# The gated MLP of a two-layer decoder trunk: from one interleaved pass to an up phase with seven block products per pair of chunks and a down phase fed from DRAM

## The chip, the cores and the metric

One core of a Trainium2 chip runs the kernel. The metric is the device time of one execution in microseconds (us). Five engines work side by side, each through its own queue in order: TensorE (PE in the profile; PEld is its weight load), VectorE (DVE), ScalarE (ACT), GpSimd (POOL) and SyncE (SP), which here issues nearly all DMA transfers.

## The reference

Two layers work on 1024 tokens of width 1024. Each adds attention and then the MLP to the residual stream. Only the MLP is changed:

```
def conv_ffn(xn, w_up, conv_w, conv_b, w_down):
    u = xn @ w_up                      # 1024 -> 2 * 2816
    c = conv_b
    for j in range(CONV_WIDTH):        # 3 taps, causal, per channel
        c = c + conv_w[j] * up[:, j:j + s]
    val, gate = jnp.split(c, 2, axis=-1)
    return (jax.nn.silu(gate) * val) @ w_down

h = h + conv_ffn(rmsnorm(h, norm_ffn[layer]), ...)
```

The 2816 hidden channels are 22 blocks of 128 rows. A block `j` has a value chunk and a gate chunk of `w_up`: a pair.

## The kernel before

Activations lie with channels on the 128 partitions and tokens along the free dimension, in two halves of 512 tokens. Every float32 product is made of three matmuls: each operand is split into a high part (rounded to the matmul's own format) and the remaining low part, and `hi*hi + hi*lo + lo*hi` is summed in one bank of PSUM (`mm3`, L162 to L164). A weight tile comes through `load_w`: DMA (L108), a rounding copy on ScalarE (`whi`, L109), a subtraction on GpSimd (`wlo`, L110).

`ffn_phase` runs behind `attention_phase` in each layer. It first ends the output projection of token half 1 (`out_final`, 24 matmuls), then the norm of that half, and then goes through the 22 pairs. For each pair, `up_half` makes four banks (two chunks, two token halves, 8 blocks of the inner dimension, 3 matmuls each: 96 matmuls). ScalarE and VectorE read each bank straight from PSUM for the convolution (L775, L777); two small instructions (L783) carry the two tokens across the border of the halves. `gate` (L788 to L793) applies the activation, multiplies on GpSimd and splits the product into `gh` and `gl`.

The down projection is interleaved: GROUPS (4, 4, 4, 4, 2, 4 pairs) are multiplied with their rows of `w_down` while the next group's pairs are made, and every group's result is added to the residual `h` from its bank (L259). Together 2112 up matmuls and 1056 down matmuls per layer. The order of the instructions on each queue is fixed when the program is built, by a scheduler; TensorE's order in the attention phase is that of the code.

Of the kernel before, what the change touches and what calls it, by code (L numbers as in the profile page):

```python
# [6 lines left out]
F32 = mybir.dt.float32  # L7
# [22 lines left out]
def trunk(ctx, tc, a, out):  # L30
# [60 lines left out]
    h_scr = [[dram.tile([P, HT], F32, name=f"hscr{c}_{h}") for h in range(2)] for c in range(KD)]  # L91
    c_scr = dram.tile([NMIX, T], F32, name="cscr")
# [93 lines left out]
    def mem_norm(l):  # L186
        mh = [qk(f"mh{i}").rearrange("p (k t) -> p k t", k=4) for i in range(2)]
        ml = [qk(f"ml{i}").rearrange("p (k t) -> p k t", k=4) for i in range(2)]
        macc = sqt("macc")
        mT = [tab(f"mT{i}").rearrange("p (k t) -> p k t", k=4) for i in range(2)]  # L190
        for i in range(2):
            nc.sync.dma_start(mT[i], a["memT"][:, 4 * i:4 * i + 4, :])
        for k in range(KD):
            square_acc(macc, mT[k // 4][:, k % 4, :], k == 0)
        rb = norm_rb(macc, psp, 2)
        mhk, mlk = (lambda k: mh[k // 4][:, k % 4, :]), (lambda k: ml[k // 4][:, k % 4, :])
        norm_split(lambda k: mT[k // 4][:, k % 4, :], rb, 3 * l + 1, mhk, mlk)
        return mhk, mlk
# [30 lines left out]
    H = {}  # L229
    PART = {}  # L230
    KORD = list(range(NPAIR - 2)) + [NPAIR, NPAIR + 1, NPAIR - 2, NPAIR - 1]

    def h_tiles(half):

        if half == 0:
            t = [big("h0", F32).rearrange("p a b -> p (a b)").rearrange("p (n t) -> p n t", n=4) for _ in range(2)]
            H[0] = lambda n: t[n // 4][:, n % 4, :]
        else:
            t = big("h1", F32).rearrange("p a b -> p (a b)").rearrange("p (n t) -> p n t", n=4)
            u = [yt("h1").rearrange("p (n t) -> p n t", n=2) for _ in range(2)]  # L240
            H[1] = lambda n: t[:, n, :] if n < 4 else u[n // 2 - 2][:, n % 2, :]

# [23 lines left out]
    def out_final(l, half, acc, psum):  # L266
# [3 lines left out]
        for n in range(KD):  # L270
            ps = psum(n)
            mm3(ps, lambda k: cols(hi)(n), lambda k: cols(lo)(n), lambda k: oh[:, c, :], lambda k: ol[:, c, :], 1)
            residual(ps, n, half, PART[l] if half else None)
            square_acc(acc, H[half](n), n == 0)
            yield n


    def attention_phase(l):
        with tc.manual_schedule(engines={mybir.EngineType.PE}):
# [207 lines left out]
            def out_last():  # L487
# [9 lines left out]
                x_split(0, rb, 3 * l + 2)  # L497
# [97 lines left out]
            if l == 0:  # L595
                MEM[0] = mem_norm(0)
                xn[0] = x_norm(0, x_load(0))
                next(xn[0])
# [142 lines left out]
    def ffn_phase(l):  # L741
        UP = ["s", "tp", "s", "tp", "s"]
        DN = ["p", "p", "o"]
# [4 lines left out]
        def norm_later(half, acc, gi):  # L748
            for rb in norm_stages(acc, psp):
                yield  # L750
            x_split(half, rb, gi)

        def normed(half, acc, gi):
            x_split(half, norm_rb(acc, psp), gi)


        h_tiles(1)
        acc = sqt("acc")
        run(out_final(l, 1, acc, lambda n: bank_of("all", ALL)))
        normed(1, acc, 3 * l + 2)  # L760


        up_st = {}

        def up_half(ci, half):
            if half == 0:
# [12 lines left out]
            if half == 0:
                nc.vector.tensor_copy(e, ps[:, HT - 2:])  # L780
            else:
                for d in (1, 2):
                    nc.vector.scalar_tensor_tensor(t[:, o:o + d], e[:, 2 - d:], w(2 - d), t[:, o:o + d],  # L783
                                                   op0=ALU.mult, op1=ALU.add)

        def gate(j):
            v, g = up_st.pop(2 * j)[2], up_st.pop(2 * j + 1)[2]
            nc.scalar.activation(g, g, AF.Silu)  # L788
            nc.gpsimd.tensor_tensor(v, v, g, op=ALU.mult)
            gh = qk("gh")  # L790
            gl = ptt("gl", [P, T])
            nc.scalar.copy(gh, v)  # L792
            nc.vector.tensor_tensor(gl, v, gh.bitcast(F32), op=ALU.subtract)  # L793
            return gh, gl

        def up(j):
            todo = [(2 * j + s, half) for s in range(2) for half in range(2)]
            if j == 0:
                todo = [(0, 0), (1, 0), (2, 0), (0, 1), (1, 1)]
            elif j == 1:  # L800
                todo = [(2, 1), (3, 0), (3, 1)]
            for ci, half in todo:
                up_half(ci, half)
            return gate(j)


        base = [sum(GROUPS[:i]) for i in range(len(GROUPS))]

        def down(gi, gt, last):
            G = GROUPS[gi]  # L810
            nb = 8 // G
            ws = {}

            def w_of(n, half):
                b = n // nb
                if (b, half) not in ws:
                    ws[b, half] = load_w(a["wd"][l, base[gi] + b])
                hi, lo = ws[b, half]
                o0 = (n % nb) * G
                return (lambda k: cols(hi)(o0 + k)), (lambda k: cols(lo)(o0 + k))  # L820

            def one(n, half):
                hs = slice(half * HT, half * HT + HT)
                ps = bank_of("all", ALL) if last else bank_of("dn", DN)
                whi, wlo = w_of(n, half if last else 0)
                mm3(ps, whi, wlo, lambda k: gt[k][0][:, hs], lambda k: gt[k][1][:, hs], G)
                residual(ps, n, half)

            if not last:
                for n in range(KD):  # L830
                    for half in range(2):
                        one(n, half)
                return
            for half in range(2):
                hs = slice(half * HT, half * HT + HT)
                acc = sqt("acc")
                for n in range(KD):
                    one(n, half)
                    square_acc(acc, H[half](n), n == 0)
                    if l == 0:  # L840
                        nc.sync.dma_start(h_scr[n][half], H[half](n))
# [117 lines left out]
```

## Time and profile before

| | us |
|---|---|
| median of 3 runs (2687.73 to 2691.45) | 2690.41 |
| profiled execution | 2691.43 |
| its span | 2689.6 |
| TensorE busy in the span | 2552.8 (95%) |
| VectorE, ScalarE, GpSimd busy | 1451.6, 1068.0, 889.3 |

The two MLP phases lie at about 622 to 1353 us and 1948 to 2673 us of the span; what is ahead of each is attention. Busy time of TensorE is not its time at peak, since its matmuls overlap: what counts is how many of them start per microsecond. A row that ends in "x4" merges neighbours, and its time then reaches from the first one's start to the last one's end, waits on the way included.

### The profile page before, as it was taken

Reading aid. Unit: us, or ns where it says so; the run is one execution under the profiler, and the core shown is the slowest. Engines: PE = TensorE matmul, PEld = TensorE weight load, DVE = VectorE, ACT = ScalarE, POOL = GpSimd, SP = SyncE. Lnnn points to the kernel's source line nnn. Section 1 sums busy time; section 2 is a strip of 40 time slices with the busy share of each in tenths; the row PEclk is TensorE's granted clock in tenths of the full one; section 3 lists DMA queues with packets and bytes.
Section 4 is the critical chain, followed back from the end, with each engine's and each line's share of the span. In section 5 each row is a group of like instructions: output and inputs, shape, how many; then the busy total and the mean of one; then the engine's idle time right before and its main releaser. Section 6 shows DMA issues by size and latency. Waiting matters only on the chain. (4 is left out here: it accounts for less than half of the span.)

```text
span 2689.6 us, 34661 instructions
## 1 busy us (share of the span) xinstructions
PE 2552.8 (95%) x12808; PEld 2133.6 (79%) x12808; DVE 1451.6 (54%) x2879; ACT 1068.0 (40%) x2077; POOL 889.3 (33%) x650
## 2 busy tenths in 40 slices
PE   5999999989999999999998898979999999999997
PEld 4878888767888888888777797867788888888886
DVE  7667777565424343434766767665554343433345
ACT  5555555544313131323355555554432222222222
POOL 5210101454323232323553333335443232233232
PEclk8899999999999999999999999999999999999999
DMA  5122223421111111111342222243211111111112
GB/s 169 48 83 56 73 62 99 145 67 64 54 49 48 48 47 51 52 47 63 121 121 62 71 66 62 71 127 105 71 48 48 53 49 48 47 48 51 52 47 94
DMA packets 103505, 187.26 MB, mean 70 GB/s; under 512 B 14236, under 2 KB 16924, under 8 KB 103336
## 3 DMA queue, kind: packets, MB, share of 16 engines
q1 hardware_dynamic: 102472, 184.36, 22.3%
q8 instruction: 101, 1.65, 0.3%
q10 hardware_dynamic: 864, 0.69, 0.1%
q14 instruction: 68, 0.56, 0.1%
HBM read 148.24 MB, written 15.78 MB: 61 GB/s over the span
## 5 line engine op out<-in xcount | busy, mean ns | idle before, releaser
L110 POOL TENSOR_TENSOR wlo<-wraw,whi 128x512 fp32r<-128x512 f32 x450 | 589.4, 1330 | 1402.1 <-ACT whi L109 1335.2
L162 PE MATMUL bk<-xh,whi 128*128 128x512 f32 x2112 | 860.7, 408 | 30.6 <-ACT xh L254 8.3
L163 PE MATMUL bk<-xl,whi 128*128 128x512 f32 x2112 | 836.4, 396 | 6.0 <-POOL xl L255 3.9
L164 PE MATMUL bk<-xh,wlo 128*128 128x512 f32 x2112 | 835.2, 395 | 0.9 <-POOL wlo L110 0.9
L109 ACT CAST whi<-wraw 128x512 fp32r<-128x512 f32 x450 | 268.2, 616 | 651.0 <-PE bk L163 448.2
L162 PEld LDWEIGHTS bk<-xh,whi 128*128 128x128 f32 x2112 | 404.5, 192 | 113.2 <-ACT xh L254 9.9
L164 PEld LDWEIGHTS bk<-xh,wlo 128*128 128x128 f32 x2112 | 403.4, 191 | 87.7 <-POOL wlo L110 1.7
L163 PEld LDWEIGHTS bk<-xl,whi 128*128 128x128 f32 x2112 | 404.3, 191 | 82.6 <-POOL xl L255 7.2
L777 DVE SCALAR_TENSOR_TENSOR gate<-bk,cw,gate 128x511 f32<-128x511 f32 (+1 forms) x176 | 131.2, 746 | 271.2 <-ACT gate L775 269.6
L162 PE MATMUL bk<-gh,whi 128*128 128x512 f32 x704 | 276.2, 393 | 1.2 <-DVE h L259 1.1
L163 PE MATMUL bk<-gl,whi 128*128 128x512 f32 x704 | 274.7, 390 | 0.0
L164 PE MATMUL bk<-gh,wlo 128*128 128x512 f32 x704 | 274.5, 390 | 0.0
L259 DVE TENSOR_TENSOR h<-h,bk 128x512 f32<-128x512 f32 x208 | 141.7, 685 | 236.5 <-PE bk L164 236.4
L388 ACT ACTIVATE y<-y,m 128x128 f32<-128x128 f32 (+1 forms) x192 | 149.3, 778 | 118.7 <-DVE m L384 116.6
L777 DVE SCALAR_TENSOR_TENSOR val<-bk,cw,val 128x511 f32<-128x511 f32 (+1 forms) x176 | 131.1, 745 | 114.6 <-ACT val L775 113.0
L399 DVE TENSOR_TENSOR ptl<-bk,pth 128x512 fp32r<-128x512 f32 (+3 forms) x288 | 152.5, 551 | 67.2 <-ACT pth L398 66.2
L398 ACT CAST pth<-bk 128x512 fp32r<-128x512 f32 (+3 forms) x288 | 131.2, 479 | 115.2 <-PE bk L397 113.5
L397 PE MATMUL bk<-ident,y 128*128 128x128 f32 x864 | 130.3, 278 | 31.4 <-DVE ptl L399 31.3
L162 PEld LDWEIGHTS bk<-gh,whi 128*128 128x128 f32 x704 | 132.5, 188 | 31.1 <-DVE h L259 2.7
L163 PEld LDWEIGHTS bk<-gl,whi 128*128 128x128 f32 x704 | 132.6, 188 | 27.8 <-issue 0.5
L164 PEld LDWEIGHTS bk<-gh,wlo 128*128 128x128 f32 x704 | 132.5, 188 | 27.7
L793 DVE TENSOR_TENSOR gl<-val,gh 128x1024 fp32r<-128x1024 f32 x44 | 53.9, 1226 | 175.5 <-ACT gh L792 175.5
(160 smaller groups left out, 3546.1 us busy)
## 6 DMA issues: line engine op xcount, KB each, us to landing
wraw<-in_wu SPq DMA_DIRECT2D x176, 256.0 KB, 2.8
wraw<-in_wd SPq DMA_DIRECT2D x104, 256.0 KB, 2.8
wraw<-in_wo SPq DMA_DIRECT2D x64, 256.0 KB, 2.8
wraw<-in_wq SPq DMA_DIRECT2D x56, 256.0 KB, 3.0
oscr<-fold SPq DMA_DIRECT2D x56, 128.0 KB, 2.3
oraw<-oscr SPq DMA_DIRECT2D x28, 256.0 KB, 3.7
cb<-cscr SPq DMA_DIRECT2D x12, 512.0 KB, 3.8
ropeqs<-roper SPq DMA_DIRECT2D x96, 64.0 KB, 2.0
```

The lines of the kernel that those rows point to most:

```text
L109: nc.scalar.copy(hi[:, w], raw[:, :n])
L110: nc.gpsimd.tensor_tensor(lo[:, w], raw[:, :n], hi[:, w].bitcast(F32), op=ALU.subtract)
L162: nc.tensor.matmul(ps, lhsT=whi(k), rhs=xhi(k), start=(first and k == 0), stop=False)
L163: nc.tensor.matmul(ps, lhsT=whi(k), rhs=xlo(k), start=False, stop=False)
L164: nc.tensor.matmul(ps, lhsT=wlo(k), rhs=xhi(k), start=False, stop=(last and k == nk - 1))
L259: nc.vector.tensor_tensor(H[half](n), (src or H[half])(n), ps, op=ALU.add)
L388: nc.scalar.activation(y[:, :nk], y[:, :nk], AF.Exp, bias=m[:, npc - 1:npc], scale=-1.0, accum_out=m[:, 2:3])
L397: nc.tensor.transpose(tp[:, jj, :], y[:, j * P:(j + 1) * P], ident)
L398: nc.scalar.copy(ph, tp[:, :nj, :])
L399: nc.vector.tensor_tensor(pl, tp[:, :nj, :], ph.bitcast(F32), op=ALU.subtract)
L777: nc.vector.scalar_tensor_tensor(t[:, o + d:o + HT], ps[:, :HT - d], w(2 - d), t[:, o + d:o + HT], op0=ALU.mult, op1=ALU.add)
L793: nc.vector.tensor_tensor(gl, v, gh.bitcast(F32), op=ALU.subtract)
```

## The change

The up projection becomes a phase of its own. The weight pair and the normed activations are each seen as a 2x2 block matrix: the weights by chunk (value, gate) and half of the inner dimension, the activations by half of the inner dimension and half of the tokens. The four result blocks come from seven block products (Strassen's scheme) in place of eight, so a pair takes 84 matmuls. The seven activation sums are made once per layer (`up_x0`, `up_x1`, `t_make`) and stay in SBUF as `t0` to `t6`. The seven weight sums are made for every pair (`prep`): loads, additions, and the high and low parts. The products' sums are put together from PSUM into a tile `u` of [128, 2, 1024] (`product`); the convolution reads `u`. The gated rows are written to DRAM (`g_scr`).

A second phase reads them back (`g_split`): first all 22 rows of token half 0 against `w_down` into eight open banks, then token half 1, with `w_down` loaded a second time. The residual is kept in DRAM meanwhile (`hf_scr`). TensorE's order is now that of the code in the MLP too. `mem_norm` of layer 1 moves into the second phase, loads its rows twice, and uses other buffers.

```diff
+        def prep(j):
+            r0, r1, r2 = (two(tab("araw")) for _ in range(3))
+            (a22, a11), (a21, a12) = ((t[:, 0, :], t[:, 1, :]) for t in (r0, r1))
+            for t, m, r in ((a22, 1, 1), (a21, 1, 0), (a11, 0, 0), (a12, 0, 1)):
+                nc.sync.dma_start(t, a["wu"][l, 2 * j + m, :, r * WC:r * WC + WC])
+            h0, l0 = map(two, w_set())
+            V.tensor_tensor(r2, r0, r1, op=ALU.add)
+            nc.scalar.copy(h0, r2)
+            G.tensor_tensor(l0, r2, h0.bitcast(F32), op=ALU.subtract)
+            h1, l1 = map(two, w_set())
+            nc.scalar.copy(h1, r0)
+            G.tensor_tensor(l1, r0, h1.bitcast(F32), op=ALU.subtract)
+            V.tensor_tensor(a21, a21, a11, op=ALU.subtract)
+            V.tensor_tensor(a12, a12, a22, op=ALU.subtract)
+            h2, l2 = (sb.tile([P, WC], R32, tag="wraw", name="adia", bufs=4) for _ in range(2))
+            V.tensor_tensor(a11, a11, a22, op=ALU.add)
+            nc.scalar.copy(h2, a11)
+            G.tensor_tensor(l2, a11, h2.bitcast(F32), op=ALU.subtract)
+            h3, l3 = map(two, w_set())
+            nc.scalar.copy(h3, r1)
+            V.tensor_tensor(l3, r1, h3.bitcast(F32), op=ALU.subtract)
...
+        def product(j, m, tags=ALL):
...
+            mm3(ps, cols(w[0]), cols(w[1]), t_k(x, 0), t_k(x, 1), 4)
...
+            if m in (2, 3):
+                st[m] = sqt("s")
+                nc.scalar.copy(st[m], ps)
+            elif m == 4:
+                V.tensor_tensor(u[:, 1, h0], ps, st[2], op=ALU.add)
+            elif m == 5:
+                V.tensor_tensor(u[:, 0, h1], ps, st[3], op=ALU.add)
+                G.tensor_tensor(st[3], st[3], st[2], op=ALU.subtract)
+            elif m == 1:
+                V.tensor_tensor(st[3], ps, st[3], op=ALU.add)
+            elif m == 6:
+                V.tensor_tensor(u[:, 1, h1], ps, st[3], op=ALU.add)
+                G.tensor_tensor(st[3], st[3], u[:, 1, h0], op=ALU.add)
+                G.tensor_tensor(st[3], st[3], u[:, 0, h1], op=ALU.subtract)
+            else:
+                V.tensor_tensor(u[:, 0, h0], ps, st[3], op=ALU.add)
+
+        def conv(j, s, u):
...
+            nc.scalar.activation(t, u[:, s, :], AF.Identity, bias=w(3), scale=w(2))
+            for d in (1, 2):
+                nc.vector.scalar_tensor_tensor(t[:, d:], u[:, s, :T - d], w(2 - d), t[:, d:], op0=ALU.mult, op1=ALU.add)
...
+            nc.gpsimd.tensor_tensor(v, v, g, op=ALU.mult)
+            nc.sync.dma_start(g_scr[l][j], v)
...
+    def up_x1(l, rb):
+        norm_in_place(l, 1, rb, (0, 1, 4, 5, 2, 3, 6, 7))
+        for c in range(2):
+            t_make(2, c, q(0, 1, c), q(1, 1, c), ALU.subtract, V, (V, G)[c])
...
+        prep(0)
+        h_tiles(1)
+        acc = sqt("acc")
+        run(out_final(l, 1, acc, lambda n: bank_of("all", ALL)))
+        prep(1)
+        st = norm_stages(acc, psp)
...
+        up_x1(l, rb)
...
+        for j in range(2, FFC):
+            if j + 1 < FFC:
+                prep(j + 1)
+            for i, m in enumerate((2, 4, 3, 5, 1, 6, 7)):
+                product(j, m)
+                if i == 0:
+                    gate(j - 1)
+        gate(FFC - 1)
+        def g_split(k, half, t):
+            raw = sqt("graw")
+            nc.sync.dma_start(raw, g_scr[l][k][:, half * HT:half * HT + HT])
+            nc.scalar.copy(t[:, 0, :], raw)
+            nc.vector.tensor_tensor(t[:, 1, :], raw, t[:, 0, :].bitcast(F32), op=ALU.subtract)
...
+        for gi, G in enumerate(GROUPS):
+            for k in range(G):
+                g_split(b0 + k, 0, gt[:, k, :, :])
+            for b in range(G):
+                hi, lo = load_w(a["wd"][l, b0 + b])
...
-        for gi, G in enumerate(GROUPS):
-            gts.append([])
-            for x in range(G):
-                gts[gi].append(up(j))
-                j += 1
-                if gi and x == (G - 1 if gi == len(GROUPS) - 1 else 0):
-                    down(gi - 1, gts[gi - 1], False)
```

Lines named below with L857 and above, up to L923, are those of the changed kernel: in `prep`, L857 adds `r2`, L859 makes `l0`, L863 `l1`, L865 and L866 the two differences, L869 `a11 + a22`, L871 `l2`, L874 `l3`; in `product`, L896, L898, L901, L903 and L907 are VectorE's sums for m = 4, 5, 1, 6, 7 and L899, L904, L905 GpSimd's three; L914 are the taps, L922 is the product of value and gate, L923 its DMA.

GpSimd's order in the MLP of layer 0 before: between two gate products (`val`) stand only the low parts of weight tiles, up and down.

```order
L789 TENSOR_TENSOR val_7757<-val_7757,gate_7828 128x1024
L110 TENSOR_TENSOR wlo_8121<-wraw_8122,whi_8120 128x512
L110 TENSOR_TENSOR wlo_8121<-wraw_8126,whi_8120 128x512
L110 TENSOR_TENSOR wlo_8187<-wraw_8188,whi_8186 128x512
L110 TENSOR_TENSOR wlo_8187<-wraw_8192,whi_8186 128x512
L789 TENSOR_TENSOR val_7905<-val_7905,gate_7976 128x1024
```

GpSimd's order at the same place after, over one pair: `s` and `u` belong to the pair being put together (`s_7076`), `alo` and `adia` to the weights of the pair two further on, `cv` to the gate.

```order
L899 TENSOR_TENSOR s_7076<-s_7076,s_7035 128x512
L859 TENSOR_TENSOR alo_7145<-araw_7139,ahi_7144 128x1024
L904 TENSOR_TENSOR s_7076<-s_7076,u_7061 128x512
L905 TENSOR_TENSOR s_7076<-s_7076,u_7061 128x512
L863 TENSOR_TENSOR alo_7150<-araw_7137,ahi_7149 128x1024
L871 TENSOR_TENSOR adia_7156<-araw_7137,adia_7155 128x512
L922 TENSOR_TENSOR cv_7184<-cv_7184,cv_7179 128x1024
L899 TENSOR_TENSOR s_7218<-s_7218,s_7177 128x512
```

The sums of the products and the weight parts of a later pair now stand in one queue, each waiting for the one ahead of it.

VectorE's order before, one chunk: all taps read a bank of PSUM (`bk`), only the two small border instructions read `edge`.

```order
L777 SCALAR_TENSOR_TENSOR val_7905<-bk_7917,cw_6332,val_7905 128x511
L777 SCALAR_TENSOR_TENSOR val_7905<-bk_7917,cw_6332,val_7905 128x510
L780 COPY edge_7916<-bk_7917 128x2
L777 SCALAR_TENSOR_TENSOR val_7905<-bk_7946,cw_6332,val_7905 128x511
L783 SCALAR_TENSOR_TENSOR val_7905<-edge_7916,cw_6332,val_7905 128x1
L777 SCALAR_TENSOR_TENSOR val_7905<-bk_7946,cw_6332,val_7905 128x510
L783 SCALAR_TENSOR_TENSOR val_7905<-edge_7916,cw_6332,val_7905 128x2
```

VectorE's order after, one pair in the steady part of the up phase, names as above.

```order
L874 TENSOR_TENSOR alo_7161<-araw_7138,ahi_7160 128x1024
L857 TENSOR_TENSOR araw_7281<-araw_7279,araw_7280 128x1024
L901 TENSOR_TENSOR s_7218<-bk_7235,s_7218 128x512
L865 TENSOR_TENSOR araw_7280<-araw_7280,araw_7279 128x512
L866 TENSOR_TENSOR araw_7280<-araw_7280,araw_7279 128x512
L903 TENSOR_TENSOR u_7203<-bk_7249,s_7218 128x512
L914 SCALAR_TENSOR_TENSOR cv_7321<-u_7203,cw_6400,cv_7321 128x1023
L907 TENSOR_TENSOR u_7203<-bk_7265,s_7218 128x512
L914 SCALAR_TENSOR_TENSOR cv_7321<-u_7203,cw_6400,cv_7321 128x1022
L869 TENSOR_TENSOR araw_7279<-araw_7279 128x512
L914 SCALAR_TENSOR_TENSOR cv_7326<-u_7203,cw_6400,cv_7326 128x1023
L914 SCALAR_TENSOR_TENSOR cv_7326<-u_7203,cw_6400,cv_7326 128x1022
```

Nine of these (all but the three that read `bk`) take both tensors from SBUF; L896 and L898 of the next pair, which read `bk`, follow, and then L874 again.

SyncE's order after, where the up phase ends: the reads of the gated rows stand behind the write of row 20 (`gscr0_20`).

```order
L114 DMA wraw_9738<-in_wd 128x512
L114 DMA wraw_9742<-in_wd 128x512
L997 DMA h0_10458<-hfscr0_0_0_109 128x512
L923 DMA gscr0_20_161<-cv_9571 128x1024
L997 DMA h0_10458<-hfscr0_1_0_111 128x512
L960 DMA graw_9686<-gscr0_0_141 128x512
L960 DMA graw_9690<-gscr0_1_142 128x512
L960 DMA graw_9694<-gscr0_2_143 128x512
```

Before, the queue held only weight loads at this place, and no transfer waited for a gate product.

## Rows read from the trace of the kernel before

**Rows 1.** The page's first part: busy us, share of the span, instructions.

```profile
PE 2552.8 (95%) x12808; PEld 2133.6 (79%) x12808; DVE 1451.6 (54%) x2879; ACT 1068.0 (40%) x2077; POOL 889.3 (33%) x650
```

**Rows 2.** Windows: both MLP phases and a quiet stretch of the first.

```profile
core 0: us, PE busy (x) PEld busy (x) DVE busy (x) ACT busy (x) POOL busy (x), PEclk, DMA share, GB/s
622.50:1353.20 730.70, 726.15 (x3194) 598.14 (x3194) 325.45 (x494) 214.59 (x323) 253.49 (x177) 1.00 0.18 59
660.00:1150.00 490.00, 490.00 (x2164) 405.73 (x2163) 194.54 (x294) 131.02 (x187) 156.47 (x109) 1.00 0.15 49
1947.80:2673.40 725.60, 722.88 (x3187) 596.02 (x3185) 309.81 (x470) 202.40 (x295) 236.97 (x164) 1.00 0.16 51
```

**Rows 3.** Page part 5, one operation's cost: busy, mean ns, idle before.

```profile
L110 POOL TENSOR_TENSOR wlo<-wraw,whi 128x512 fp32r<-128x512 f32 x450 | 589.4, 1330 | 1402.1 <-ACT whi L109 1335.2
...
L109 ACT CAST whi<-wraw 128x512 fp32r<-128x512 f32 x450 | 268.2, 616 | 651.0 <-PE bk L163 448.2
...
L259 DVE TENSOR_TENSOR h<-h,bk 128x512 f32<-128x512 f32 x208 | 141.7, 685 | 236.5 <-PE bk L164 236.4
...
L777 DVE SCALAR_TENSOR_TENSOR val<-bk,cw,val 128x511 f32<-128x511 f32 (+1 forms) x176 | 131.1, 745 | 114.6 <-ACT val L775 113.0
...
L793 DVE TENSOR_TENSOR gl<-val,gh 128x1024 fp32r<-128x1024 f32 x44 | 53.9, 1226 | 175.5 <-ACT gh L792 175.5
```

**Rows 4.** Groups of instructions by line, the same columns.

```profile
L789 POOL TENSOR_TENSOR val<-val,gate 128x1024 f32<-128x1024 f32 x44 | 105.7, 2402 | 90.9 <-ACT gate L788 90.9
...
L775 ACT ACTIVATE val<-bk,cw 128x512 f32<-128x512 f32 x88 | 68.2, 775 | 40.9 <-PE bk L164 40.9
...
L788 ACT ACTIVATE gate<-gate 128x1024 f32<-128x1024 f32 x44 | 46.7, 1061 | 99.2 <-DVE gate L783 99.2
...
L792 ACT CAST gh<-val 128x1024 fp32r<-128x1024 f32 x44 | 46.2, 1050 | 108.2 <-POOL val L789 108.2
...
L152 DVE SCALAR_TENSOR_TENSOR xn<-h,gains,bk 128x512 f32<-128x512 f32 x48 | 33.5, 738 | 2.1 <-DMA vk<-kmn 1.5 <-PE bk L135 0.6
```

**Rows 5.** Timeline of VectorE and GpSimd around 48 us: start us, us, instruction.

```profile
44.33 6.79 POOL L110 TENSOR_TENSOR wlo<-wraw,whi 128x512 fp32r<-128x512 f32 x4
...
45.25 8.02 DVE L145 TENSOR_TENSOR xacc<-xacc,sq 128x512 f32<-128x512 f32 x6
```

**Rows 6.** Instructions of line 783 (both inputs in SBUF): ns min/median/max, forms.

```profile
L783 DVE SCALAR_TENSOR_TENSOR val<-edge,cw,val x88: 200/930/1327, 649.4 to 2596.6; 128x1 f32<-128x1 f32 x44, 128x2 f32<-128x2 f32 x44
```

**Rows 7.** Timeline around 664 us: the two engines in the MLP itself.

```profile
648.13 2.53 POOL L110 TENSOR_TENSOR wlo<-wraw,whi 128x512 fp32r<-128x512 f32 x2 [5.52 <-ACT whi L109]
...
663.56 1.81 POOL L110 TENSOR_TENSOR wlo<-wraw,whi 128x512 fp32r<-128x512 f32 x1 [0.43 <-ACT whi L109]
...
663.00 1.22 DVE L793 TENSOR_TENSOR gl<-val,gh 128x1024 fp32r<-128x1024 f32 x1 [0.45 <-ACT gh L792]
664.14 1.25 DVE L783 SCALAR_TENSOR_TENSOR val<-edge,cw,val 128x2 f32<-128x2 f32 x1
```

**Rows 8.** Line 145 (both inputs in SBUF): ns min/median/max.

```profile
L145 DVE TENSOR_TENSOR acc<-acc,sq x56: 686/693/1649, 560.2 to 2675.0; 128x512 f32<-128x512 f32 x56
```

**Rows 9.** Page part 6, DMA issues: KB each, median us to landing.

```profile
wraw<-in_wu SPq DMA_DIRECT2D x176, 256.0 KB, 2.8
...
oraw<-oscr SPq DMA_DIRECT2D x28, 256.0 KB, 3.7
```

**Rows 10.** Page part 2, GB/s in 40 slices of the span.

```profile
GB/s 169 48 83 56 73 62 99 145 67 64 54 49 48 48 47 51 52 47 63 121 121 62 71 66 62 71 127 105 71 48 48 53 49 48 47 48 51 52 47 94
```

**Rows 11.** Timeline of TensorE after a wait of 2.55 us.

```profile
554.49 0.50 PE L162 MATMUL bk<-xh,whi 128*128 128x512 f32 x1 [2.55 <-ACT xh L410]
...
555.94 0.63 PE L162 MATMUL bk<-xh,whi 128*128 128x512 f32 x1
556.37 0.63 PE L163 MATMUL bk<-xl,whi 128*128 128x512 f32 x1
...
558.50 0.63 PE L162 MATMUL bk<-xh,whi 128*128 128x512 f32 x1
558.93 0.44 PE L163 MATMUL bk<-xl,whi 128*128 128x512 f32 x1
```

More of the change, by code (lines that the diff above doesn't have):

```diff
@@ L229, in trunk @@
     H = {}
+    HC = {}
     PART = {}
@@ L595, in attention_phase @@
             if l == 0:
-                MEM[0] = mem_norm(0)
+                run(mem_norm(0))
                 xn[0] = x_norm(0, x_load(0))
@@ L746, in ffn_phase, with w_set @@
         nc.sync.dma_start(cw, a["cw"][:, l])
[L748 to L754, printed above, removed]
+        V, G = nc.vector, nc.gpsimd
+        A = {}
+        sets = itertools.cycle("wpwpw")
+        def w_set():
+            if next(sets) == "w":
+                return (sb.tile([P, 1024], R32, tag="whi", name="ahi", bufs=3),
+                        sb.tile([P, 1024], R32, tag="wlo", name="alo", bufs=3))
+            return ptt("ahi", [P, 1024]), ptt("alo", [P, 1024])
@@ L786, in gate @@
[L786 to L804, printed above, removed]
@@ L807, in ffn_phase @@
-        base = [sum(GROUPS[:i]) for i in range(len(GROUPS))]
[L809 to L829, printed above, removed]
-                for n in range(KD):
-                    for half in range(2):
-                        one(n, half)
-                return
[L834 to L841, printed above, removed]
-                if l == 0:
-                    if half == 0:
-                        normed(half, acc, 3)
-                    else:
-                        NEXT.append(norm_later(1, acc, 3))
-                    continue
-                rb = norm_rb(acc, psp)
-                for k in range(KD):
-                    nc.vector.scalar_tensor_tensor(H[half](k), H[half](k), gains[:, 6, k:k + 1], rb,
-                                                   op0=ALU.mult, op1=ALU.mult)
-                    nc.sync.dma_start(out[:, k, hs], H[half](k))
@@ new lines, in ffn @@
+        rb = next(st)
+        product(1, 4, B6)
+        up_x1(l, rb)
+        for m in (3, 5, 1, 6):
+            for j in range(2):
+                product(j, m, B6)
+        product(0, 7)
+        prep(2)
+        gate(0)
+        product(1, 7)
+        for j in range(2, FFC):
[6 more added lines that the diff above has]
+        gate(FFC - 1)
@@ new lines, in finish, with after @@
+        def finish(n, half, ps, acc):
+            residual(ps, n, half)
+            square_acc(acc, H[half](n), n == 0)
+            if l == 0:
+                nc.sync.dma_start(h_scr[n][half], H[half](n))
+        def after(half, acc):
+            for rb in norm_stages(acc, psp):
+                yield
+            if l == 0:
+                x_split(half, rb, 3)
+                return
+            for k in range(KD):
+                nc.vector.scalar_tensor_tensor(H[half](k), H[half](k), gains[:, 6, k:k + 1], rb, op0=ALU.mult, op1=ALU.mult)
+                nc.sync.dma_start(out[:, k, half * HT:half * HT + HT], H[half](k))
@@ L862, in ffn_phase @@
+        nx = after(1, acc)
         if l == 0:
-            MEM[1] = mem_norm(1)
-        down(len(GROUPS) - 1, gts[-1], True)
+            NEXT.append(nx)
+        else:
+            run(nx)
     for l in range(2):
```

212 lines of the change are left out of this document (169 added, 43 removed).

## The prediction

> **What bounds the kernel now.** The page's busy times come first: TensorE is busy 95% of the span, VectorE 54%, ScalarE 40%, GpSimd 33% [rows 1]. Windows over the MLP say more: both phases run at the full clock, 1.00, that is 2.4 GHz, and in the quiet stretch 2164 matmuls start in 490.00 us, one each 0.2264 us [rows 2]. A layer's 3168 MLP matmuls take 717.3 us at that pace, and the phases last 730.7 and 725.6 us. So TensorE bounds the MLP almost alone, with 13 and 8 us of waiting. The other three engines are busy under half of it, and so the page shows their work as free. The change fills them, so the cost of one operation on each is read next [rows 3, 4], and then what VectorE and GpSimd do to each other [rows 5 to 8].
>
> **What it removes.** 12 of 96 matmuls in each of 44 pairs: 528 x 0.2264 = 119.5 us. A pair takes 84 x 0.2264 = 19.02 us, a layer 2904 matmuls, 657.5 us. Were everything else hidden, the MLPs would give back all of it. The border instructions (L783) and GpSimd's work for the down weights leave the up phase too, but these were hidden.
>
> **What a pair now asks of the other engines.** Durations: GpSimd 1.265 us for 512 columns (two in 2.53 [rows 7]) and 2.40 for 1024; VectorE 0.69 for 512 columns, both inputs in SBUF [rows 8], 1.23 for 1024, 0.685 when one input is a bank; a tap of 1023 columns 0.745 + 512 x 1.04 ns = 1.28, the slope from 0.69 and 1.23. ScalarE 0.62 and 1.05 per copy, 1.06 for the activation, and 0.775 + 512 x 0.85 ns = 1.21 for the start of a tap, its slope from the copies. Per pair:
> - GpSimd: `l0`, `l1`, gate product at 2.40; `l2` and three sums at 1.265: 12.26 us.
> - VectorE: two of 1.23, three of 0.69, four taps of 1.28, all with both inputs in SBUF: 9.65; five sums out of banks: 3.43.
> - ScalarE: three copies of 1.05, three of 0.62, two tap starts, the activation: 8.5.
>
> Each alone fits into 19.02 us. The trace says that the first two don't run at the same time. Around 48 us VectorE adds two SBUF tiles again and again while GpSimd makes low parts: six additions in 8.02 us, 1.34 each in place of 0.69, four subtractions in 6.79, 1.70 each in place of 1.265 [rows 5]. In the MLP itself, an instruction on one column, 0.20 us alone, takes up to 1.33 and 0.93 in the median [rows 6], ending with GpSimd's instruction, and GpSimd's 1.265 become 1.81 behind an `L793` [rows 7]. The taps that read banks and the sums out of banks show no such thing: their means stay at 0.745 and 0.685 [rows 3]. After the change all four taps read `u`, in SBUF.
>
> One exchange costs 1.70 us where the two durations add up to 1.96: 0.13 of overlap at each change of sides. So a pair's 16 such instructions need at least 12.26 + 9.65 - 16 x 0.13 = 19.8 us, more than TensorE's 19.02, if one of the two is always ready.
>
> The Trainium skill, "SBUF — State Buffer", section "Who interferes with whom", has this as an exclusive lock for the whole instruction: a VectorE instruction with two SBUF inputs against a GpSimd instruction that reads SBUF, the second waiting until the first is done. The trace agrees that they exclude each other, not quite that they do for all of both durations (1.70, not 1.96). By the rule a pair would need 21.9 us.
>
> **The loop of the steady part.** The order of the two queues decides how much is left idle. From the end of `l3` (L874), t = 0, one pair goes: GpSimd L899 to 1.1; VectorE's sum `r2`, which waits for it, to 2.2; ScalarE's copy to 3.4; VectorE's L901, L865, L866, the last one holding up GpSimd to 3.9; `l0` to 6.3; the first tap gets in ahead of L904, which ends at 8.6; L905 9.9; the last bank's sum (L907) 10.7; `l1` has started at 9.9 and ends at 12.3, the second tap waits for it, 13.4; L869 14.0; activation and copy 15.2; now GpSimd's `l2` waits for the last two taps and ends at 17.6; L896 and L898 17.6; the gate product takes 17.6 to 20.0, and `l3` of the next pair waits for that: 21.05. Each hand-over is taken at 0.09 us. Without the exclusion the same list closes in 15 us and TensorE's 19.02 would rule. I take 21.05; from below it is 19.8, from above the 21.9 and the 1.2 us in which this list leaves both idle, 23.1. TensorE waits 2.03 us a pair, mostly for a bank: its eight banks are held until L907 and ScalarE's copy behind `h2`. The loop rules from pair 3 or 4 on, 18 times a layer: 36.5 us.
>
> **The other terms, per layer.**
> - Start, 21 us (bounds 10 and 30). `up_x1` has eight normings of 0.74 [rows 4], then ten additions and ten low parts of 1024 columns, shared by VectorE and GpSimd, which must alternate. GpSimd has two additions for `t5` and `t6` queued ahead of the low part of `t2` that product 3 wants: it is ready 17.6 us after the norm, where TensorE has 2.7 us of work. Product 1 of pair 1 waits for a tile `u`, which comes free after `t5`. Pairs 0 and 1 end 59 us behind `out_final`, against 38 for their 168 matmuls. Before, half 0's chunks hid that norm.
> - `out_final` late, 4 us (0 to 6): `prep(0)` holds two of the three `whi` buffers, and its `l3` and `prep(1)`'s `l0` stand ahead of the last output weights.
> - From up to down, 9 us (2 to 15): the reads of gated rows stand behind the write of row 20 on SyncE; that write comes some 15 us after the last `l3`, and 3.7 us [rows 9], a copy and a low part follow, where TensorE ends its products 11 us after that `l3`.
> - Down phase, 3 us (0 to 20): 1056 matmuls as before. Half 0 moves 1.05 MB per 24 matmuls, 5.43 us: 193 GB/s. The highest slice shown has 169 [rows 10]; I take it as carried, since nothing there shows a limit.
>
> Moved `mem_norm` and the extra stores of `h` lie beside matmuls: 0, a few us if not. ScalarE's waits hold back only copies whose banks are counted above.
>
> **Sum.** 657.5 + 36.5 + 21 + 4 + 9 + 3 = 731 us per layer, 1462 for both, against 730.7 + 725.6 = 1456.3: 6 us more. On the profiled execution's 2691.4 that makes 2697, say 2698 (1 above the median of the runs). The gain of 119.5 is eaten by 73 of the loop, 42 of the start and the rest. What a measurement of this kernel can tell from no change is about 0.2%, 5.4 us.
>
> **The rivals.**
> - *The exclusion is absorbed.* If VectorE's turns fall into gaps that GpSimd has anyway (waiting for ScalarE's copies), the pair is TensorE's, 19.2: 36 x 1.85 = 67 us less, and 5 less at each start: 2621. For it: GpSimd is idle twice per pair in my list. Against it: 19.8 us of turns in 19.02. Faster begins at a loop of about 20.7 us. Chance 0.20.
> - *It costs all of both durations*, and the idle pieces remain: 23.1 a pair, 36 x 2.05 = 74 more: 2772, slower. For it: the median of 0.93 for an instruction of 0.20 [rows 6]. The skill's rule above would give this time. Chance 0.17.
> - *Gated rows bound the down phase*: at 169 GB/s a chunk takes 6.2 us, 0.77 x 22 x 2 = 34 more: 2732. For it: nothing before moves more. Against it: DMA is busy only 0.15 to 0.18 at 49 to 59 GB/s [rows 2]. Chance 0.09.
> - *The clock falls.* After a wait of 2.55 us, matmuls start 0.43 us apart, the 1.2 GHz level, until 558.9 [rows 11]: about eight, 1.6 us lost. One such fall in each pair, 19.02 + 1.6 = 20.6, still fits the loop; if the lower level lasts until the phase's granted clock is 0.83, a pair takes 19.02 / 0.83 = 22.9 us and the sum comes to 2765. Chance 0.06.
>
> My own case has 0.48; with the bounds of its terms it reaches from 2665 to 2735.
>
> **How the numbers follow.** Likeliest: 2698. The range goes to the first rival's near part and to the second's and fourth's: 2640 to 2772. Faster by over 5.4 us: the first rival's 0.20 and 0.13 of my case, 0.33. Within: 0.12 of mine and 0.01, 0.13. Slower: 0.23 of mine, 0.17, 0.08, 0.06: 0.54.
>
> **What will show it.** Matmuls in a pair's stretch: 84 in about 21 us, VectorE and GpSimd together busy for nearly all of it, waits included. L914 at a mean well over 1.28, L859 and L863 over 2.40, L901 at 0.69. TensorE waiting for VectorE or ScalarE (banks) once a pair, and for over 10 us in the `up_x1` of each layer. Wrong would be: L914 at 1.28 while GpSimd works, or an up phase near 420 us and yet no gain, whose cause would then be in the down phase.

## The result, and the profile after

The changed kernel takes 2755.74 us in the median (2748.07 to 2757.88), the kernel before 2689.07 beside it: a ratio of 1.0242, with an interval of 1.0220 to 1.0264. The forecast was 2698 us in a range of 2640 to 2772: slower, as the likeliest sign had it, and 58 us further. The profiled execution took 2757.88 us, its span 2756.1.

First the page of the changed kernel: busy us and shares, then groups of instructions (mean ns of one ahead of the second bar).

```profile
PE 2472.4 (90%) x12280; PEld 2043.9 (74%) x12280; DVE 1818.4 (66%) x2776; ACT 1201.5 (44%) x2189; POOL 1325.4 (48%) x812
...
L914 DVE SCALAR_TENSOR_TENSOR cv<-u,cw,cv 128x1023 f32<-128x1023 f32 (+1 forms) x176 | 333.2, 1895 | 56.7 <-ACT cv L912 55.2
...
L859 POOL TENSOR_TENSOR alo<-araw,ahi 128x1024 fp32r<-128x1024 f32 x44 | 125.5, 2853 | 88.2 <-ACT ahi L858 69.2
```

Against [rows 1], TensorE has 528 matmuls and 80 us less, VectorE 367 us more in 103 instructions fewer, GpSimd 436 us more. The taps, all from SBUF now, take 1.895 us where 1.28 was reckoned without GpSimd [rows 3 for those from banks], `l0` 2.85 in place of 2.40.

Next the windows of both layers, which answer to [rows 2]: the first two pairs, the other twenty, the wait between the phases, half 0 and half 1 of the down phase. The first two numbers are the stretch and its length, the last three the granted clock, DMA's share and GB/s.

```profile
642.20:708.20 66.00, 46.86 (x180) 36.59 (x178) 54.73 (x48) 21.67 (x26) 32.82 (x15) 0.84 0.11 40
708.20:1122.90 414.70, 386.10 (x1679) 313.85 (x1680) 342.82 (x274) 160.27 (x181) 288.75 (x139) 1.00 0.21 73
1122.90:1132.20 9.30, 0.40 (x2) 0.00 (x0) 2.71 (x4) 1.86 (x4) 6.00 (x4) 0.73 0.63 199
1132.20:1264.60 132.40, 127.12 (x528) 101.58 (x528) 61.66 (x65) 57.04 (x100) 69.35 (x48) 0.95 0.68 224
1264.60:1402.30 137.70, 124.40 (x544) 102.52 (x545) 32.93 (x47) 39.33 (x74) 67.51 (x56) 0.95 0.37 118
2002.80:2065.50 62.70, 45.76 (x180) 36.13 (x179) 52.00 (x45) 21.63 (x25) 31.68 (x14) 0.84 0.10 35
2065.50:2482.40 416.90, 387.95 (x1681) 314.80 (x1679) 342.39 (x276) 160.33 (x182) 292.37 (x140) 1.00 0.21 74
2482.40:2492.30 9.90, 0.35 (x3) 0.01 (x1) 2.67 (x5) 1.79 (x4) 6.00 (x4) 0.66 0.66 224
2492.30:2618.30 126.00, 122.90 (x528) 99.92 (x529) 60.86 (x64) 56.22 (x97) 69.54 (x47) 0.99 0.65 216
2618.30:2739.80 121.50, 121.50 (x539) 100.22 (x537) 21.92 (x25) 28.28 (x52) 52.50 (x45) 1.00 0.30 98
```

Twenty pairs in 414.7 and 416.9 us, where 84 matmuls of 0.2264 us would need 380.4. In the trace a pair's L874 follows the last one's by 21.0 us; TensorE's mean over the twenty is 20.7 and 20.8, because a few of the first still start 19.0 to 19.7 us apart. TensorE is at the full clock there and waits once per pair. The waits of TensorE from 760 to 1050 us (us in total, times, longest):

```profile
PE bk L168 <- ACT s L894: 23.2, 14, 1.7
```

The copy named there is the last link. What makes it late is seen on the timeline of VectorE and GpSimd in the steady part (start us, us, instruction):

```profile
898.64 2.40 POOL L922 TENSOR_TENSOR cv<-cv 128x1024 f32<-128x1024 f32 x1 [1.16 <-DVE cv L914]
901.01 2.26 POOL L899 TENSOR_TENSOR s<-s 128x512 f32<-128x512 f32 x1
...
899.68 2.44 DVE L874 TENSOR_TENSOR alo<-araw,ahi 128x1024 fp32r<-128x1024 f32 x1
902.16 2.19 DVE L857 TENSOR_TENSOR araw<-araw 128x1024 f32<-128x1024 f32 x1
904.28 0.68 DVE L901 TENSOR_TENSOR s<-bk,s 128x512 f32<-128x512 f32 x1
...
905.52 2.90 POOL L859 TENSOR_TENSOR alo<-araw,ahi 128x1024 fp32r<-128x1024 f32 x1 [2.25 <-ACT ahi L858]
908.39 2.27 POOL L904 TENSOR_TENSOR s<-s,u 128x512 f32<-128x512 f32 x1
910.73 1.29 POOL L905 TENSOR_TENSOR s<-s,u 128x512 f32<-128x512 f32 x1
...
917.20 1.28 POOL L871 TENSOR_TENSOR adia<-araw,adia 128x512 fp32r<-128x512 f32 x1 [2.81 <-ACT adia L870]
...
920.68 2.44 DVE L874 TENSOR_TENSOR alo<-araw,ahi 128x1024 fp32r<-128x1024 f32 x1
```

Add start and length: the ends are 901.04 (GpSimd), 902.12 (VectorE), 903.27 (GpSimd), 904.35 (VectorE). Each comes 1.08 to 1.15 us after the other engine's. About half of each recorded length of L874, L899 and L857 is waiting for a turn. L901, with one input in a bank, keeps its 0.68. By the Trainium skill, "SBUF — State Buffer", section "Who interferes with whom", such a pair of instructions excludes each other for the whole instruction. The trace agrees, but for the 0.1 us or so by which each turn is shorter than the instruction alone.

The loop is the forecast's, so the missing 61 us of the profiled execution lie elsewhere. From the windows, the forecast's terms and the delays outside the MLPs:

| place | forecast, us late | measured |
|---|---|---|
| twenty pairs of the loop, per layer | 36.5 | 34.3 and 36.5 |
| first two pairs (38.0 of work) | 21 | 28.0 and 24.7 |
| wait between the phases | 9 | 9.3 and 9.9 |
| half 0 (119.5 of work) and half 1 (121.5, with the norms' matmuls) | 3 | 12.9 + 16.2, and 6.5 + 0 |
| attention's end and `out_final` | 4 | 8.7 and 5.9 |
| `mem_norm(0)` at the start of the kernel | 0 | 9.9 to 10.9 |

TensorE's first matmul, ahead of everything in the kernel, shows the last row: it waits for `macc`, which came at 8.75 us before. The second row is TensorE inside half 1 of layer 0, at `mem_norm(1)`.

```profile
18.66 1.01 PE L131 MATMUL bk<-ones,macc 128*128 128x1 f32 x4 [18.66 <-DVE macc L151]
...
1345.32 0.98 PE L131 MATMUL bk<-ones,macc 128*128 128x1 f32 x4 [13.26 <-DVE macc L151]
```

### The profile page after: what moved, and what is told of

Its sections match the earlier page's. It is cut to its first block, busy times and chain, and to the rows that moved or that the text cites. A ratio compares the mean times of both kernels' runs of the same rounds, so it can differ in the third digit from the quotient of the medians.

```text
span 2756.1 us, 34584 instructions
## 1 busy us (share of the span) xinstructions
PE 2472.4 (90%) x12280; PEld 2043.9 (74%) x12280; DVE 1818.4 (66%) x2776; ACT 1201.5 (44%) x2189; POOL 1325.4 (48%) x812
## 5 line engine op out<-in xcount | busy, mean ns | idle before, releaser
L168 PE MATMUL bk<-t,ahi 128*128 128x512 f32 x1056 | 421.1, 399 | 72.3 <-ACT s L894 57.2
L169 PE MATMUL bk<-t,ahi 128*128 128x512 f32 x1056 | 415.7, 394 | 11.7 <-DVE t L333 11.7
L170 PE MATMUL bk<-t,alo 128*128 128x512 f32 x1056 | 414.5, 392 | 0.0
L914 DVE SCALAR_TENSOR_TENSOR cv<-u,cw,cv 128x1023 f32<-128x1023 f32 (+1 forms) x176 | 333.2, 1895 | 56.7 <-ACT cv L912 55.2
L168 PE MATMUL bk<-xh,whi 128*128 128x512 f32 x704 | 313.0, 445 | 30.9 <-ACT xh L277 8.6
L168 PEld LDWEIGHTS bk<-t,ahi 128*128 128x128 f32 x1056 | 200.7, 190 | 131.0 <-ACT s L894 72.4
L169 PE MATMUL bk<-xl,whi 128*128 128x512 f32 x704 | 289.0, 411 | 9.7 <-POOL xl L278 4.7
L170 PE MATMUL bk<-xh,wlo 128*128 128x512 f32 x704 | 287.4, 408 | 4.6 <-POOL wlo L116 4.6
L169 PEld LDWEIGHTS bk<-t,ahi 128*128 128x128 f32 x1056 | 200.7, 190 | 53.7 <-DVE t L333 12.7
L168 PEld LDWEIGHTS bk<-xh,whi 128*128 128x128 f32 x704 | 140.4, 199 | 60.4 <-ACT xh L277 10.2
L485 ACT CAST pth<-bk 128x512 fp32r<-128x512 f32 (+3 forms) x288 | 131.1, 478 | 116.4 <-PE bk L484 114.7
L859 POOL TENSOR_TENSOR alo<-araw,ahi 128x1024 fp32r<-128x1024 f32 x44 | 125.5, 2853 | 88.2 <-ACT ahi L858 69.2
L169 PEld LDWEIGHTS bk<-xl,whi 128*128 128x128 f32 x704 | 140.2, 199 | 34.8 <-POOL xl L278 8.9
L170 PEld LDWEIGHTS bk<-xh,wlo 128*128 128x128 f32 x704 | 138.9, 197 | 36.3 <-POOL wlo L116 5.5
```

The source lines that it names most:

```text
L168: nc.tensor.matmul(ps, lhsT=whi(k), rhs=xhi(k), start=(first and k == 0), stop=False)
L169: nc.tensor.matmul(ps, lhsT=whi(k), rhs=xlo(k), start=False, stop=False)
L170: nc.tensor.matmul(ps, lhsT=wlo(k), rhs=xhi(k), start=False, stop=(last and k == nk - 1))
L485: nc.scalar.copy(ph, tp[:, :nj, :])
L859: G.tensor_tensor(l0, r2, h0.bitcast(F32), op=ALU.subtract)
L914: nc.vector.scalar_tensor_tensor(t[:, d:], u[:, s, :T - d], w(2 - d), t[:, d:], op0=ALU.mult, op1=ALU.add)
```

## The experiments

My theory: VectorE and GpSimd take turns, so that the lengths of their lists add; this sets the 21.0 us loop, and GpSimd "helps" at a loss. Rivals: a late copy on ScalarE holds the banks; GpSimd is a parallel helper, and VectorE is simply full; the place of three GpSimd instructions between two sums of one pair makes the chain long, wherever else GpSimd works.

**All seven GpSimd instructions of a pair on VectorE.**

```diff
-            G.tensor_tensor(l0, r2, h0.bitcast(F32), op=ALU.subtract)
+            V.tensor_tensor(l0, r2, h0.bitcast(F32), op=ALU.subtract)
...
-            nc.gpsimd.tensor_tensor(v, v, g, op=ALU.mult)
+            nc.vector.tensor_tensor(v, v, g, op=ALU.mult)
```

(So too `l1`, `l2`, L899, L904, L905.)

> The seven GpSimd instructions of a pair (three subtractions in prep, three in product, the gate product) are VectorE's, nothing else is changed. My theory: VectorE and GpSimd hold each other up, so a pair's list runs in turns and GpSimd's work costs more there than it would on VectorE. Then VectorE alone has some 17.7 us of work a pair, under TensorE's 19.0, L914 falls from 1.90 us to about 1.28, the pitch of a pair falls from 21.0 us to 19.0 to 19.4, and the kernel from 2756 to about 2690 us (2680 to 2700). Rival: GpSimd is a parallel helper and VectorE's durations of now are its own. Then VectorE gets 6.6 us or more on top of 17.4 us a pair, the pitch rises to 24 us, and the kernel takes about 2870 us.

2630.21 us, ratio to before 0.9772 (0.9757 to 0.9787): 125.5 us less than the changed kernel, twice what I expected. The same lines and windows in this kernel:

```profile
L914 DVE SCALAR_TENSOR_TENSOR cv<-u,cw,cv 128x1022 f32<-128x1022 f32 (+1 forms) x176 | 230.2, 1322 | 0.1
...
PE 2442.4 (93%) x12280; PEld 2038.8 (78%) x12280; DVE 1841.6 (70%) x3084; ACT 1211.6 (46%) x2189; POOL 680.9 (26%) x504
```

```profile
636.20:697.90 61.70, 46.45 (x179) 36.91 (x178) 52.49 (x56) 21.70 (x27) 16.55 (x6) 0.83 0.10 34
697.90:1078.50 380.60, 380.60 (x1681) 315.14 (x1680) 362.71 (x423) 169.19 (x188) 6.07 (x4) 1.00 0.26 91
1078.70:1200.10 121.40, 120.18 (x530) 98.90 (x528) 57.28 (x61) 54.51 (x97) 64.27 (x45) 1.00 0.69 227
```

VectorE executes 308 instructions more, worth 44 x (3 x 1.23 + 4 x 0.70) = 286 us, and its busy time rises by 23. So some 262 us, at least, of the 1818 that the page of the changed kernel calls busy were waits. The twenty pairs take 380.6 us, TensorE's own time without a gap. And three other losses shrink with the loop: the first two pairs by 4.3 us, the wait between the phases from 9.3 to 0.2, half 0 from 132.4 to 121.4, at 227 GB/s. So at this rate the gated rows' transfers did not bound the down phase. The rival "VectorE is full" expected 2870 us and falls. The whole 125.5, over both layers: loop 70, waits between the phases 19, half 0 17, attention's ends 12, first pairs 7. Of the 12, layer 1's 5.7 are not clear of chance: its attention takes from 589 to 600 us in kernels whose attention is the same.

**The copies that free two banks, on VectorE.**

```diff
-                nc.scalar.copy(st[m], ps)
+                V.tensor_copy(st[m], ps)
```

> The two copies a pair that free a bank onto ScalarE (L894, named by the trace as what TensorE waits for once a pair) are VectorE's. Rival theory, a late copy on ScalarE behind h2 holds the banks: the copy comes sooner, the pitch falls towards 19.2 us and the kernel to about 2695 us. My theory, the list of VectorE and GpSimd is what is late and the copy only the last link: two more instructions of 0.69 us in that list, the pitch stays at 21.0 or rises to 22.4 us, and the kernel takes 2755 to 2810 us.

2785.37 us, 30 more than the changed kernel; the pitch (from one pair to the next) is 21.5. TensorE still waits, now for VectorE directly (760 to 1050 us):

```profile
PE bk L168 <- DVE u L896: 12.2, 13, 1.0
PE bk L168 <- DVE s L894: 12.2, 13, 0.9
```

ScalarE's copy was not the cause: the releaser that a trace names is only the last link.

**Only `product`'s three on VectorE, and its counterpart, only `prep`'s and the gate's four.**

```diff
-                G.tensor_tensor(st[3], st[3], st[2], op=ALU.subtract)
+                V.tensor_tensor(st[3], st[3], st[2], op=ALU.subtract)
```

> Of the changed kernel, only the three 512-wide subtractions and additions of product (L899, L904, L905), which stand between two sums of the same pair, are VectorE's; prep's and the gate's four instructions stay on GpSimd. Turns (the two engines hold each other up wherever they work, and the lengths of both lists add): VectorE has 13.7 us a pair and GpSimd 8.5 us by the durations that each has alone (1.23 and 0.70 us against 2.40 and 1.26 us); the sum of 22.2 less the 2.9 us that the same sum is too high for the changed kernel gives a pitch of 19.3 us (19.0 to 20.3) and some 2650 us (2635 to 2690). Rival, the chain: it is GpSimd's place between two sums that makes the banks late, wherever else it works; then this edit alone gives all that moving everything gave, 19.0 us and 2630 to 2640 us, and its counterpart gives nothing.

> The counterpart: prep's three subtractions and the gate product are VectorE's, and product's three instructions between the sums stay on GpSimd. Turns: 16.0 us on VectorE and 3.8 us on GpSimd, 19.8 less up to 2.9 us: under TensorE's 19.0 us or just at it, the pitch is 19.0 to 19.5 us and the kernel takes 2630 to 2650 us. The chain: the instructions that make the banks late are all still there, the pitch stays near 21 us and the kernel near 2750 us.

2719.29 us (ratio 1.0103, 1.0078 to 1.0128) at a pitch of 20.2 in the mean, and 2667.98 us (0.9917, 0.9901 to 0.9933) with TensorE's pairs 19.04 us apart at first and 19.3 towards the end. Both pitches lie in the ranges that turns give, neither where the chain put it: the three instructions between the sums are worth 36 us, the four elsewhere 88. The twenty pairs of layer 0 in each, and the wait behind them in the second:

```profile
706.30:1106.90 400.60, 390.56 (x1680) 312.56 (x1680) 392.01 (x335) 159.69 (x182) 188.72 (x80) 1.00 0.21 77
```

```profile
696.10:1079.00 382.90, 382.46 (x1680) 314.65 (x1680) 341.49 (x353) 160.29 (x181) 119.72 (x61) 1.00 0.22 81
1079.00:1087.70 8.70, 0.39 (x3) 0.03 (x1) 4.99 (x6) 1.94 (x5) 4.87 (x3) 0.69 0.60 201
```

In the loop alone the two edits gain 27 and 64 us over both layers, together more than the 70 of all seven, since TensorE's own time is the floor; that the whole gains add up to 124 of 125.5 is chance. Both times lie above the ranges that I gave (to 2690 and to 2650): I took the all-VectorE kernel's time and put the loop on top, as if the other losses went too. They don't: in the second kernel the loop loses only 2.5 and 3.8 us, yet the wait between the phases stays at 8.7 and 9.7 us and half 0 at 131.1 and 126.6, as its list of 19.3 us is still longer than TensorE's 19.02 and so still ends late. Of the 38 us between it and the all-VectorE kernel, 6 are the loop's. The timeline of that second kernel shows the turns with one GpSimd instruction only:

```profile
911.99 2.20 POOL L899 TENSOR_TENSOR s<-s 128x512 f32<-128x512 f32 x1 [9.06 <-DVE u L898]
...
911.83 1.21 DVE L874 TENSOR_TENSOR alo<-araw,ahi 128x1024 fp32r<-128x1024 f32 x1
913.07 2.19 DVE L857 TENSOR_TENSOR araw<-araw 128x1024 f32<-128x1024 f32 x1
915.19 0.68 DVE L901 TENSOR_TENSOR s<-bk,s 128x512 f32<-128x512 f32 x1
```

L874 was first and has its 1.21 us undisturbed. L899 starts 0.16 later and ends 1.15 after L874's end. L857 starts at 913.07 and ends 1.07 after L899's end.

**The norm of the memory rows as before for layer 0, one more step for layer 1.**

```diff
+        if l == 0:
+            mT = [four(tab(f"mT{i}")) for i in range(2)]
+            for i in range(2):
+                nc.sync.dma_start(mT[i], a["memT"][:, 4 * i:4 * i + 4, :])
...
                 square_acc(macc, t[:, x, :], k + x == 0)
+        yield
...
-                if (n, b) in ((4, 0), (5, 0), (5, 2)):
+                if (n, b) in ((3, 2), (4, 2), (5, 0), (5, 2)):
```

> The norm of the memory rows is put back to its old form for layer 0 (whole loads, read once), and for layer 1 a step is put between the squares and the norm's matmul, some 6 us of down-projection apart. If the 10 us by which everything starts late and the 13.7 us wait in half 1 of layer 0 are real losses: 2756 falls by 10 and by 12 to about 2733 us (2728 to 2740). Rival: the late start is made up where attention waits for other things, and the wait in half 1 moves to the next step: 2745 us or more.

2729.43 us (1.0137, 1.0122 to 1.0152), 26 less. `macc` comes at 8.90 us, and in half 1 of layer 0 TensorE doesn't wait for it (20 us earlier in the span, 12 of them because all of half 1 starts earlier):

```profile
8.90 1.01 PE L131 MATMUL bk<-ones,macc 128*128 128x1 f32 x4 [8.90 <-DVE macc L151]
...
1325.49 0.50 PE L131 MATMUL bk<-ones,macc 128*128 128x1 f32 x4
```

Both losses were real, and neither had been given back. The one kernel undoes both, so it doesn't tell what the double loads cost apart from the small buffers.

**The first gated rows read during the last pair; then also the row writes on GpSimd's DMA queue.**

```diff
+                if j == FFC - 1 and 2 <= i < 6:
+                    if i == 2:
+                        early.append(sb.tile([P, 4, 2, HT], R32, tag="xh0", name="g0"))
+                    g_split(i - 2, 0, early[0][:, i - 2, :, :])
```

```diff
-            nc.sync.dma_start(g_scr[l][j], v)
+            nc.gpsimd.dma_start(g_scr[l][j], v)
```

> The first four gated rows of the down-projection are read and split during the last pair instead of behind its gate. If the wait between the phases is only this chain: the gaps of 9.3 and 9.9 us go, and with them some of the lower clock after them: 20 to 30 us less, 2726 to 2736 us. Rival: the gated rows come late by the DMA queue anyway, and the wait appears at the second group of rows: at most 8 us less, 2748 us or more.

> The changed kernel with the first four gated rows of the down-projection read during the last pair, and with the row writes (L923) on GpSimd's DMA queue, so that no read stands behind a write on SyncE's queue. Theory: the wait of 9.3 and 9.9 us between the phases was the write of pair 20, which waits for that pair's gate product on GpSimd and has the reads of the rows behind it on SyncE's queue; then the rows are read some 14 us sooner, the waits fall to 3 us or less, and the kernel to 2735 to 2744 us. Rival: the lists of VectorE and GpSimd are a pair behind anyway, and the banks of the last pair, or the weights of the down-projection, keep TensorE waiting as long: 2748 us or more.

2750.78 us (1.0222, 1.0207 to 1.0237) and 2757.78 us (1.0250, 1.0228 to 1.0272): 5 less and 2 more than the changed kernel, nothing that counts. In the first the waits were 9.3 and 11.1 us. In the second they were 6.6 and 7.2, 2.7 less in each layer, but half 0 took 132.8 and 132.0 us, in layer 1 six more than before the edit. SyncE's queue in the first (start, time until issued), where the reads (L931) still stand behind row 20's write (L923):

```profile
1125.88 0.33 SPq L923 DMA_DIRECT2D gscr<-cv  x1
1126.26 0.42 SPq L1002 DMA_DIRECT2D h<-hfscr  x1
1126.73 1.77 SPq L931 DMA_DIRECT2D graw<-gscr  x3
```

And in the second, where no write is ahead of them any more, the longest waits of SyncE's queue from 1095 to 1130 us:

```profile
SPq L114 <- POOL wlo L116: 22.2, 2, 20.3
SPq L114 <- PE bk L170: 9.5, 1, 9.5
```

The reads now wait behind weight loads, whose buffers come free when GpSimd has split earlier weights (20.3 us) or TensorE has used them (9.5). What the wait hangs on is mostly not which transfer heads the queue but that the lists end late. With only `product`'s three on GpSimd, row 20 is still written behind TensorE's last product (1079.0):

```profile
1082.92 0.33 SPq L923 DMA_DIRECT2D gscr<-cv  x1
```

In the all-VectorE kernel, with its queue in the old order, it is written ahead of the last product (1078.5):

```profile
1067.64 0.33 SPq L923 DMA_DIRECT2D gscr<-cv  x1
1068.02 1.75 SPq L960 DMA_DIRECT2D graw<-gscr  x3
```

**Both savings; and then also the activations' sums on VectorE, all seven instructions or only the five of `up_x1`.**

```diff
-            t_make(4, c, q(0, 0, c), q(1, 1, c), ALU.add, (V, G)[c], (V, V)[c])
+            t_make(4, c, q(0, 0, c), q(1, 1, c), ALU.add, V, V)
```

> All seven GpSimd instructions of a pair on VectorE, and the memory rows' norm in its old form for layer 0 and with one more step for layer 1. The two savings lie in different stretches, so they add: 2630 less 26 is 2604 us (2600 to 2610). Rival: they share a cover (an earlier loop meets the norm's wait at another step): 2612 us or more.

> As the kernel with both savings, and the seven GpSimd instructions that build the sums of the activations at the start of each layer's up-projection are VectorE's too. If turns decide there as well: five of the seven lie in the second half's part, each costs 2.40 us on GpSimd and 1.23 on VectorE, so up to 5.9 us a layer are saved of the 12.7 us that TensorE waits there: 2592 to 2602 us beside 2604. Rival, GpSimd is a real second engine in this stretch: VectorE gets 6 to 9 us more and the start is that much later, 2612 to 2620 us.

> As the kernel with both savings (pair on VectorE, norm of the memory rows put back), and of the activations' sums only those of the second half (the five GpSimd instructions of up_x1) on VectorE. The version with all seven moved spent 0.3 and 2.2 us less in the up phases and 5 to 6 us more a layer ahead of them. If it is the two of the first half, made beside attention's end where VectorE is busy, that cost this: the up phases keep the 440 us, nothing is lost ahead of them, 2600 to 2604 us. Rival: the loss ahead of the phases has another cause: 2608 us or more.

Both savings: 2603.66 us (0.9668, 0.9651 to 0.9686), they add. All seven of the start as well: 2610.28 (0.9699, 0.9684 to 0.9713), 6.6 more, where I expected a gain; the two intervals just touch. Only the five: 2599.09 us (0.9661, 0.9645 to 0.9678), the fastest of all, though the 4.6 us to 2603.66 are less than these intervals can tell; the 11.2 us to 2610.28 are clear of them. The profiles say where: the up phases (first product to last) take 440.3 and 442.1, 440.0 and 439.9, 438.6 and 436.8 us in the three. What the version with all seven lost lies ahead of them (1.6 and 6.3 us), where `up_x0` runs beside attention's end. The wait there (560 to 660 us) in that kernel, and in the one with both savings; layer 1 has the same, 7.0 against 2.4 us, and the version with only the five has 2.4 in both layers:

```profile
PE bk L168 <- DVE hp L583: 7.1, 1, 7.1
```

```profile
PE bk L168 <- DVE hp L583: 2.4, 2, 1.8
```

So VectorE is what attention's end waits for, and there two instructions are cheaper on GpSimd, turns or not. The Trainium skill, "Perfetto Trace Analysis", section "Optimizing Scalar/DVE Operations", says that offloading between these two engines might not help. In the loop it didn't (125.5 us back for undoing it); at this place it did (6.6 us lost by undoing it).

## Why the prediction was right, and where it was short

- **The time is inside the range partly by luck.** My own case reached from 2665 to 2735, and 2755.74 lies outside it. The range went on to 2772 only for the second and fourth rivals, and neither came true: the pair took 21.0 us and not 23.1, at a granted clock of 1.00. The sign and the loop were right by their mechanism; the 61 us beyond the sum are other terms, below.
- **The loop was right in its steps, not only in its sum.** The list said 21.05 us, with L899 ending 1.1 after L874, `r2` 2.2, `l0` 6.3, L904 8.6, L905 9.9. The trace has 21.0, and 1.15, 2.23 (the rows above) and 6.3, 8.5, 9.9. One step was wrong: `l2` (L871) got in ahead of the last tap and ended at 16.4, where I had it wait to 17.6; the last tap then waited for it, and the gate product ended at 19.9 against 20.0. L914 stood at 1.895, "well over 1.28". That turns cause it, and that GpSimd's share of them is what pushes the pair over 19.02, is shown by the three kernels that move it away, in parts and in whole. "The exclusion is absorbed" (2621) needed 19.2 a pair in the changed kernel and had 21.0. "It costs all of both durations" (2772) came near the time by accident: it needed 23.1. The turns don't show its mark, the whole sum of both durations.
- **The wait of 9 us from up to down** had its size (9.3 and 9.9) and its place, row 20's write, but not its nature. I told it as a chain of transfers; taking that write off the queue shortened the wait by 2.7 us a layer and the kernel not at all, since the weights that GpSimd splits are late by then too. Nor does the wait shrink with the loop's loss: it is still 8.7 and 9.7 us where the list takes 19.3 us, and goes (0.2) only where the list fits into TensorE's time.
- **"Moved `mem_norm` and the extra stores of `h` lie beside matmuls: 0" failed, 27 us in all** (measured by the kernel that undoes it, 26). For layer 0 there are no matmuls beside it: it is the first thing in the kernel, and its loads go twice through a ring of small buffers. For layer 1 the squares and the matmul that needs them were put in one step, and with TensorE's order fixed, TensorE stood for 13.3 us.
- **"Down phase, 3 us (0 to 20)" and "`out_final` late, 4 us (0 to 6)" were mis-sized.** Half 0 lost 12.9 and 6.5 us, attention's ends 8.7 and 5.9. With GpSimd out of the pair, half 0 takes 121.4 and 119.7 us, and the ends give back 6 each. I had costed them without turns and without the backlog that the loop leaves behind; in half 0 of layer 0 the clock, granted at 0.95 after the wait, was part of it. Layer 1's 5.9 stays open: the kernel that undoes the norm gives back 5.0 of it too, and that stretch varies by as much. DMA, which the third rival feared at 169 GB/s, carried 224 and 227.
- **"Start, 21 us (10 to 30)"** was 28.0 and 24.7, within its bounds; the granted clock was 0.84 there, which the term left out.

Together: +11 and +16 for the norm, +7 for attention's ends, +13 for half 0, +11 for the starts, -1 for the loop and the waits, and +4 for the norms' matmuls in half 1, which the forecast's 657.5 left out, make the 61 us between the sum's 2697 and 2757.88.

## What to carry to other kernels

Count VectorE instructions with two SBUF inputs and GpSimd instructions as one list: if the two lists together exceed what TensorE needs, work given to GpSimd is lost, because here it takes twice as long there (2.40 against 1.23 us) and stops VectorE meanwhile; where VectorE is the late engine and has other work, a little on GpSimd still pays. A list that outlasts TensorE by a tenth does not cost that tenth alone: buffers come free a pair late, and the next phase's start, its clock and its first half pay again, so undoing it here was worth 125 us where the loop accounts for 70. A list that is longer by 0.3 us (19.3 against 19.02) pays nearly the same there: the wait was 8.7 us in place of 9.3. Work that is "hidden beside matmuls" needs those matmuls named, above all at the start of a kernel and where TensorE's order is fixed.

## What the runs showed of the hardware

- In turns, an instruction ends 1.07 to 1.15 us after the other engine's end, where alone it takes 1.21 to 1.26: some 0.1 us of each is done before the turn comes. The forecast's 0.13, read from 512 columns [rows 5], holds for 1024 too.
- Waiting for a turn is recorded as busy time: at least 262 us of VectorE's 1818. A page's busy share of VectorE or GpSimd is no measure of their work when both are in use; the mean of one instruction against its lone length is.
- Half 0 of the down phase ran at 227 GB/s with DMA engines busy 0.69 of the time and no wait of TensorE for them.
